# A smaller descriptor ring for GpSimd's transfers, and its memory given to one more probability tile of each kind and one more slot

## The chip, the cores and the metric

One core of one Trainium2 chip runs the kernel; the other cores are idle. The metric is the device time of one execution in microseconds (us). Engines are named as in the profile: PE (TensorE, the matrix unit) with its weight loads PEld, DVE (VectorE), ACT (ScalarE), POOL (GpSimd) and SP (SyncE, which only issues transfers here). Each engine runs its own instructions in the order in which the program has them, and waits where a semaphore says so.

## The reference, cut to what matters

One layer of a decoder over 1024 tokens of width 1024: a wide projection, three attention branches (a: dilated windows in three groups, b: compressed, selected and windowed blocks, c: a window of 128 with sinks), a gated sum of the three, an output projection and a layer norm. All in float32.

```python
h = x @ w_in[l] + b_in[l]
...
s = jnp.einsum('bnikgd,bnckd->bnkgic', qp.astype(jnp.float32), kc.astype(jnp.float32)) * ATTN_SCALE
s = s - (slopes.reshape(Hkv, G)[:, :, None, None] * dist_scale) * dist.astype(jnp.float32)
s = jnp.where(valid[None, :, None, None], s, NEG)
lse = jax.nn.logsumexp(s, axis=-1)
...
p = jnp.exp(s - lse[..., None])
o = jnp.einsum('bnkgic,bnckd->bnikgd', p, vc.astype(jnp.float32))
...
merged = (mg[:, :, 0] * (ya @ w_branch[l, 0])
          + mg[:, :, 1] * (yb @ w_branch[l, 1])
          + mg[:, :, 2] * (yc @ w_branch[l, 2]))
y = (merged @ w_out[l]).astype(x.dtype)
x = layer_norm(DEEPNORM_ALPHA * x + y, ln_g[l], ln_b[l])
```

## The kernel before, in words

The first 885 us or so are the **dense stage**: the projection, with its own pool of on-chip memory, and its results stored to memory on the chip's HBM. Then that pool is closed and the pool "ab" opened, with which all the rest works: branch a (head pairs p = 0 to 3, each with blocks b = 0 to 7), then branch c, then branch b, then the output projection. While branch c runs, PE's gaps are filled with the products of branch a's output with its branch weights (tile `dbr`, and `ma` for the gated sums), and while branch b runs with those of branch c; so a branch's outputs are needed again as soon as the next branch begins.

The work of one block and head pair is a *unit* with three parts, `front`, `mid` and `back` (`a_unit`, `b_unit`, `c_unit`). `front` puts scores into a PSUM bank (PE, L931 and L943 for a, L1029 for b and c); DVE adds the distance strip, takes the row's least value and writes the sum into a **probability tile** ("softmin", L681, tiles `ae`, `be`, `ce`); ACT exponentiates in place (L685); DVE or ACT scales by the reciprocal of the row sum (L690, L692). `mid` transposes the probabilities on PE (L970 and L972 for a, L1176 for c, L1139 for b; tiles `atp`, `atq`, `ctp`, `btp`) and copies them back into the slots (L163 on ACT, L165 on DVE; `apt`, `pt`). `back` multiplies them with the values (PE, L987, L994, L1070) and gates the result (`y`, L700 on DVE), which GpSimd stores to memory with its own transfers (L703). The lo parts of a split float32 operand are made on POOL (L179) from the hi parts that DVE or ACT casts (L173, L171).

Four things of the pool matter here. `slot` hands out 4 KB slots (tag "g", `NG` of them; queries, keys, values and transposed probabilities). `etile` hands out probability tiles of two kinds (tags "e0" and "e1", `NE` of each; an a or c unit takes one of each, its two heads, and a b unit two of each). A score bank is one of `NPS` = 4. A tile is handed out again when its last reader is done, and whoever writes it next waits for that reader: for a probability tile the reader is the transpose on PE, and the writer is DVE's softmin, or POOL's fill of the masked columns ahead of it (L928, `MEMSET`) or its copy of the sink (L1164).

The parts of the units are written down with two lags (`LAG_MID`, `LAG_BACK`), but the order of each engine's instructions is decided when the program is built, by the framework's scheduler, which plays the program with its own idea of durations and takes what is ready first; when a tile comes free is one of its inputs. So a change of the number of tiles can reorder every engine.

GpSimd issues 82 transfers in all: the stores of `y` of the three branches (`y_a` 8, `y_b` and `y_c` 16 each), of the merged sums `m` (40, L778) and two of `h`. Its descriptors go through a ring in on-chip memory, by default 16 KB of each partition. The program gives these transfers eight completion semaphores in turn, and a transfer on one of them waits for the one before it there, so that at most eight are under way. All other transfers are issued by SP and don't use this ring.

Of the kernel before, what the change touches and what calls it, by code (L numbers as in the profile page):

```python
# [101 lines left out]
B_STRIP = SEL_W + P + CMP_W  # L102


NG, NH, NE, NPS = 23, 36, 4, 4
LAG_MID, LAG_BACK = 3.5, 2.0
NWOP = 9
C1, C2 = 2, 4
# [1196 lines left out]
def build(arrays):  # L1305
    import concourse.bacc as bacc

    nc = bacc.Bacc("TRN2", target_bir_lowering=False, num_devices=1)
    args = [nc.dram_tensor(f"in_{n}", a.shape, mybir.dt.from_np(a.dtype), kind="ExternalInput").ap()
            for n, a in arrays.items()]  # L1310
    out = nc.dram_tensor("out_0", (S, D), F32, kind="ExternalOutput").ap()
    with tile.TileContext(nc, schedule_with_timeline_sim=True) as tc:
        trunk(tc, *args, out)
    return nc
# [39 lines left out]
```

## Time and profile before

| what | value |
|---|---|
| median of 3 runs | 1614.71 us (1611.72, 1614.71, 1619.58) |
| the profiled execution | 1612.14 us, of which 1610.3 us are its span (first to last instruction) |
| PE busy | 1565.2 us, 97% of the span |
| DVE, ACT, POOL busy | 61%, 48%, 41% |
| mean granted clock of PE | 0.992 |
| chain of waits | PE 85%, DVE 8%, issue 3%, ACT 2%, DMA 1% |

Busy shares are over the whole span; the dense stage, with more than half of it, is PE alone, and what lies behind it has other limits in other places. A stretch in which PE's busy time is near its length is bounded by PE; the difference is all that another arrangement of the work could give there, as long as PE's own work stays the same. The granted clock is a share of 2.4 GHz; 0.50 in a stretch is the lower level, 1.2 GHz.

### The profile page before, as it was taken

Reading aid. Unit: us, or ns where it says so; the run is one execution under the profiler, and the core shown is the slowest. Engines: PE = TensorE matmul, PEld = TensorE weight load, DVE = VectorE, ACT = ScalarE, POOL = GpSimd, SP = SyncE. Lnnn points to the kernel's source line nnn. Section 1 sums busy time; section 2 is a strip of 40 time slices with the busy share of each in tenths; the row PEclk is TensorE's granted clock in tenths of the full one; section 3 lists DMA queues with packets and bytes.
Section 4 is the critical chain, followed back from the end, with each engine's and each line's share of the span. In section 5 each row is a group of like instructions: output and inputs, shape, how many; then the busy total and the mean of one; then the engine's idle time right before and its main releaser. Section 6 shows DMA issues by size and latency. Waiting matters only on the chain.

```text
span 1610.3 us, 26460 instructions
## 1 busy us (share of the span) xinstructions
PE 1565.2 (97%) x9468; PEld 1260.1 (78%) x9468; DVE 978.8 (61%) x2325; ACT 774.4 (48%) x1628; POOL 659.3 (41%) x613
## 2 busy tenths in 40 slices
PE   8999999999999999999999999998989999999997
PEld 8888888888899988788788666766767767776786
DVE  8533335555733444844873777776586787778655
ACT  5444444444322233533543566664574576668422
POOL 0655555555555655565663101135335412210320
PEclk9999999999999999999999999999999999999999
DMA  4322332333443322522544776767536522312632
GB/s 163 131 105 105 123 119 112 118 131 131 172 129 112 105 105 105 209 105 105 209 171 182 258 252 215 244 228 241 191 112 229 190 105 62 125 65 92 230 124 79
DMA packets 104004, 241.08 MB, mean 150 GB/s; under 512 B 11456, under 2 KB 28608, under 8 KB 103872
## 3 DMA queue, kind: packets, MB, share of 16 engines
q1 hardware_dynamic: 98208, 221.56, 39.0%
q0 software_dynamic: 5664, 17.83, 2.9%
q8 instruction: 75, 1.23, 0.3%
q14 instruction: 57, 0.47, 0.1%
HBM read 154.94 MB, written 84.41 MB: 149 GB/s over the span
## 4 chain that ended last, share of the span: by engine, by line
PE 85%; DVE 8%; issue 3%; ACT 2%; DMA 1%; POOL 0%; SPq 0%; DVEq 0%; ACTq 0%; POOLq 0%
PE dn L192 13%; PE dn L190 13%; PE dn L191 13%; PE vn L491 8%; PE pv L1070 6%; PE bs L1029 4%; PE btp L1139 4%; PE dbr L190 3%; PE dbr L191 3%; PE dbr L192 3%; PE do L1227 2%; PE do L1226 2%; PE do L1228 2%; PE apv L994 1%; DVE ae L681 1%
## 5 line engine op out<-in xcount | busy, mean ns | idle before, releaser
L223 POOL TENSOR_TENSOR s<-s,s 128x512 fp32r<-128x512 f32 x147 | 201.8, 1374 | 267.3 <-ACT s L222 262.4
L190 PE MATMUL dn<-xh_t,s 128*128 128x512 f32 x456 | 177.6, 389 | 0.0
L192 PE MATMUL dn<-xh_t,s 128*128 128x512 f32 x456 | 177.5, 389 | 0.0
L191 PE MATMUL dn<-xl_t,s 128*128 128x512 f32 x456 | 177.4, 389 | 0.0
L223 POOL TENSOR_TENSOR a<-w,a 128x512 fp32r<-128x512 f32 x109 | 146.8, 1347 | 57.0 <-ACT a L222 41.1
L222 ACT CAST a<-w 128x512 fp32r<-128x512 f32 x114 | 70.8, 622 | 167.0 <-PE dn L192 133.3
L685 ACT ACTIVATE be<-be,mn 128x64 f32<-128x64 f32 (+8 forms) x192 | 115.2, 602 | 52.3 <-DVE mn L681 51.6
L190 PE MATMUL dn<-xh_b,a 128*128 128x512 f32 x288 | 113.4, 394 | 5.6 <-ACT c L412 5.6
L222 ACT CAST s<-s 128x512 fp32r<-128x512 f32 x152 | 93.8, 619 | 51.1 <-PE dn L192 34.0
L230 DVE TENSOR_TENSOR s<-w,s 128x512 f32<-128x512 f32 x38 | 30.5, 803 | 141.5 <-POOL s L223 139.7
L192 PE MATMUL dn<-xh_b,a 128*128 128x512 f32 x288 | 113.2, 393 | 0.0
L191 PE MATMUL dn<-xl_b,a 128*128 128x512 f32 x288 | 113.2, 393 | 0.0
L190 PEld LDWEIGHTS dn<-xh_t,s 128*128 128x128 f32 x456 | 85.7, 188 | 17.8
L192 PEld LDWEIGHTS dn<-xh_t,s 128*128 128x128 f32 x456 | 85.7, 188 | 17.8
L191 PEld LDWEIGHTS dn<-xl_t,s 128*128 128x128 f32 x456 | 85.6, 188 | 17.8
L1139 PE MATMUL btp<-ident,be 128*128 128x128 f32 x592 | 87.8, 279 | 2.4 <-DVE be L690 1.8
L228 DVE TENSOR_TENSOR s<-w 128x512 f32<-128x512 f32 x38 | 33.0, 867 | 84.1 <-POOL s L223 81.5
L1139 PEld LDWEIGHTS btp<-ident,be 128*128 128x128 f32 x592 | 68.3, 142 | 19.5 <-issue 8.0
L432 POOL TENSOR_TENSOR o<-c,c 128x512 f32<-128x512 f32 x38 | 64.9, 1708 | 26.0 <-issue 16.6
L681 DVE CUSTOM_DVE_ANT_0 be<-bs,con_b 128x512 f32<-128x512 f32 (+5 forms) x128 | 66.2, 530 | 8.0 <-PE bs L1029 7.9
L190 PEld LDWEIGHTS dn<-xh_b,a 128*128 128x128 f32 x288 | 54.7, 190 | 17.8 <-ACT c L412 6.4
L685 ACT ACTIVATE ae<-ae,mn 128x768 f32<-128x768 f32 (+2 forms) x64 | 51.8, 811 | 34.0 <-DVE mn L681 31.4
(309 smaller groups left out, 4258.2 us busy)
## 6 DMA issues: line engine op xcount, KB each, us to landing
w<-in_w SPq DMA_DIRECT2D x88, 512.0 KB, 4.4
h<-o SPq DMA_DIRECT2D x47, 512.0 KB, 3.7
h<-hi SPq DMA_DIRECT2D x38, 512.0 KB, 2.7
a<-h SPq DMA_DIRECT2D x48, 256.0 KB, 7.5
h<-gt SPq DMA_DIRECT2D x12, 512.0 KB, 2.6
h<-vo SPq DMA_DIRECT2D x24, 256.0 KB, 2.8
av<-h SPq DMA_DIRECT2D x12, 512.0 KB, 5.6
xr<-in_xt SPq DMA_DIRECT2D x8, 512.0 KB, 6.7
```

Of the source, the lines that this page charges most:

```text
L190: nc.tensor.matmul(ps, h, mh[k], start=(first and k == 0), stop=False, skip_group_check=True)
L191: nc.tensor.matmul(ps, h, ml[k], start=False, stop=False, skip_group_check=True)
L192: nc.tensor.matmul(ps, l, mh[k], start=False, stop=(last and k == n - 1), skip_group_check=True)
L222: nc.scalar.copy(hi[o], v)
L223: e.tensor_sub(lo[o], v, hi[o].bitcast(F32))
L432: nc.gpsimd.tensor_add(d, e, half(o2, 1, k2, tm["c5"])[1])
L491: nc.tensor.matmul(to, x_[b][k][:, at], w_[a][:, :, c], start=(first and t_ % 2 == k == i == 0), stop=(last and k == 3 and i == 2), skip_g ...
L681: nc.vector.tensor_tensor_reduce(e, ps, strip, scale, init, OP.add, OP.min, m)
L685: nc.scalar.activation(e, e, AF.Exp, bias=m, scale=-1.0, accum_out=den)
L1029: nc.tensor.matmul(pss[s], qs[s][:, bl], ks[2 * i + s][:, c0:c0 + n], start=(i == 0), stop=(i == 1))
L1070: nc.tensor.matmul(pv[64 * s:64 * s + 64, :, b % 2], v[s], state[b, s, j // w][:, j % w], start=(j == 0), stop=(j == len(vs) - 1), skip_gr ...
L1139: nc.tensor.transpose(tp[:, j], e[:, k:k + P], ident)
```

## The change

The ring of descriptors of GpSimd's transfers is 4096 bytes of each partition, not 16384. The 12 KB that come free hold one more slot (4 KB) and one more probability tile of each of the two kinds (4 KB for e0, whose largest tile has 1024 columns, 3 KB for e1, whose largest has 768). Nothing else in the text of the kernel changes.

```diff
-NG, NH, NE, NPS = 23, 36, 4, 4
+NG, NH, NE, NPS = 24, 36, 5, 4
...
-    nc = bacc.Bacc("TRN2", target_bir_lowering=False, num_devices=1)
+    nc = bacc.Bacc("TRN2", target_bir_lowering=False, num_devices=1, dynamic_dma_scratch_size=4096)
```

The order of the dense stage is the same on every engine. Behind it the scheduler orders the work otherwise in many places. Three of them follow.

**Branch a, head pair 2, DVE.** The rows stand where the last output of head pair 1 (`y_8618`) is gated between the softmins of head pair 2's blocks 4 and 5. `as1` are scores of the two dilated groups, `as0` those of the near group. Before:

```order
L681 ISA ae_8626,mn_8622<-as0_8647,ast21_8315,mn_8622 128x256
L681 ISA mn_8622 128x1
L165 COPY apt0_8500<-atp_8501 128x128
L165 COPY apt2011_8499<-atp_8508 128x128
L700 TENSOR_TENSOR y_8618<-apv11_8569,ag1_7705 128x4x4x32
L681 ISA ae_8685,mn_8682<-as0_8707,ast20_8311,mn_8682 128x256
L681 ISA mn_8682 128x1
L956 RECIPROCAL rc_8624<-den_8623 128x2
L690 TENSOR_SCALAR ae_8626<-ae_8626,rc_8624 128x768
L165 COPY apt2010_8498<-atp_8561 128x128
L681 ISA ae_8686,mn_8682<-as1_8688,ast21_8315 128x2x192
```

After the change, the same place:

```order
L681 ISA ae_8626,mn_8622<-as0_8647,ast21_8315,mn_8622 128x256
L681 ISA mn_8622 128x1
L681 ISA ae_8686,mn_8682<-as1_8688,ast21_8315 128x2x192
L681 ISA mn_8682 128x1
L165 COPY apt0_8500<-atp_8501 128x128
L165 COPY apt2011_8499<-atp_8508 128x128
L690 TENSOR_SCALAR ae_8518<-ae_8518,rc_8517 128x512
L681 ISA ae_8685,mn_8682<-as0_8707,ast20_8311,mn_8682 128x256
```

The softmin of block 5's second head (`as1_8688`) now stands ahead of two copies, the gate `y_8618` and a scale, and a scale of an older block (`ae_8518`) has come behind it: the softmins go first, the older blocks' scales and copies later.

**From branch a to branch c, DVE.** Here DVE casts branch a's outputs and weights (`wha1`) for the first branch products, copies the selected keys for branch b (`bsk`, L1018), and takes the softmins of branch c (`ce`). Before:

```order
L1018 COPY bsk0_11101<-kc0_408 128x64
L681 ISA ce_10175,mn_10170<-cs_10173,con_c_7667,nsink_66 128x256
L681 ISA mn_10170 128x1
L1018 COPY bsk1_11102<-kc1_409 128x64
L1168 RECIPROCAL rc_10133<-den_10132 128x2
L173 CAST wha1_10058<-wra1_10057 128x512
L690 TENSOR_SCALAR ce_10136<-ce_10136,rc_10133 128x256
L690 TENSOR_SCALAR ce_10137<-ce_10137,rc_10133 128x256
L681 ISA ce_10176,mn_10170<-cs_10174,con_c_7667,nsink_66 128x256
L681 ISA mn_10170 128x1
L1018 COPY bsk2_11103<-kc2_410 128x64
```

After the change:

```order
L1018 COPY bsk0_11101<-kc0_408 128x64
L1018 COPY bsk1_11102<-kc1_409 128x64
L1168 RECIPROCAL rc_10133<-den_10132 128x2
L173 CAST wha1_10058<-wra1_10057 128x512
L690 TENSOR_SCALAR ce_10136<-ce_10136,rc_10133 128x256
L690 TENSOR_SCALAR ce_10137<-ce_10137,rc_10133 128x256
L1018 COPY bsk2_11103<-kc2_410 128x64
L681 ISA ce_10175,mn_10170<-cs_10173,con_c_7667,nsink_66 128x256
L681 ISA mn_10170 128x1
L1018 COPY bsk3_11104<-kc3_411 128x64
L681 ISA ce_10176,mn_10170<-cs_10174,con_c_7667,nsink_66 128x256
```

The softmin of `cs_10173` has moved behind the cast of `wha1`, the two scales and a copy, and that of `cs_10174` behind two copies more. Fewer rows stand ahead of `wha1`, more ahead of the two softmins.

**From branch c to branch b, PE.** `dbr_11537` is the first of branch c's branch products, which needs DVE's cast `yhc0_11481`; `btp` are transposes of branch b's probabilities, `bs1` and `bs2` scores. Before:

```order
L1139 MATMUL btp_11396<-ident_63,be2_11266 128x128
L190 MATMUL dbr_11537<-yhc0_11481,whc0_11466 128x512
L1029 MATMUL bs1_11561<-bsk0_11101,bq100_11130 128x448
L1029 MATMUL bs1_11561<-bsk2_11103,bq100_11130 128x448
L1029 MATMUL bs1_11562<-bsk1_11102,bq110_11133 128x448
L1029 MATMUL bs1_11562<-bsk3_11104,bq110_11133 128x448
L1029 MATMUL bs2_11571<-bwk0_11113,bq100_11130 128x384
L1029 MATMUL bs2_11571<-bwk2_11115,bq100_11130 128x384
L1139 MATMUL btp_11447<-ident_63,be1_11340 128x128 x2
```

After the change:

```order
L1139 MATMUL btp_11396<-ident_63,be2_11266 128x128
L1139 MATMUL btp_11447<-ident_63,be1_11340 128x128 x2
L1139 MATMUL btp_11447<-ident_63,be2_11341 128x128 x2
L1139 MATMUL btp_11453<-ident_63,be2_11341 128x128
L1139 MATMUL btp_11456<-ident_63,be1_11342 128x128 x2
L1139 MATMUL btp_11456<-ident_63,be2_11343 128x128 x2
L190 MATMUL dbr_11537<-yhc0_11481,whc0_11466 128x512
L1029 MATMUL bs1_11561<-bsk0_11101,bq100_11130 128x448
```

Nine transposes of the next block now stand ahead of the branch product. On DVE the five scales on which these transposes wait (`be1_11340` to `be2_11343`, L690) stand ahead of the cast `yhc0_11481`, and before they stood right behind it.

## Rows read from the trace of the kernel before

**Rows 1.** The page: the chain that ended last, by engine.
```profile
PE 85%; DVE 8%; issue 3%; ACT 2%; DMA 1%; POOL 0%; SPq 0%; DVEq 0%; ACTq 0%; POOLq 0%
```

**Rows 2.** Stretches: length; busy PE, PEld, DVE, ACT, POOL; PE clock, DMA share, GB/s.
```profile
935.00:983.00 48.00, 46.86 (x718) 35.21 (x720) 32.11 (x137) 26.97 (x71) 4.05 (x14) 1.00 0.64 227
983.00:1022.00 39.00, 36.26 (x530) 26.86 (x522) 27.57 (x112) 24.25 (x65) 4.38 (x14) 1.00 0.72 242
1022.00:1062.00 40.00, 38.33 (x416) 28.36 (x416) 27.95 (x106) 27.04 (x76) 4.72 (x19) 1.00 0.44 150
1062.00:1100.00 38.00, 31.16 (x166) 23.28 (x166) 32.42 (x113) 22.95 (x79) 20.28 (x38) 0.91 0.80 292
1100.00:1172.00 72.00, 71.66 (x394) 53.40 (x392) 41.72 (x146) 38.28 (x121) 26.36 (x61) 1.00 0.67 223
1172.00:1200.00 28.00, 23.73 (x137) 16.82 (x135) 25.55 (x128) 22.79 (x87) 8.58 (x9) 0.94 0.23 81
1200.00:1480.00 280.00, 276.54 (x1687) 199.56 (x1688) 210.99 (x748) 178.46 (x458) 79.18 (x83) 1.00 0.35 114
```

**Rows 3.** The same view in stretches of 20 us, branch a.
```profile
980.00:1000.00 20.00, 17.82 (x245) 12.27 (x244) 19.54 (x81) 17.74 (x47) 2.12 (x7) 1.00 0.44 144
1000.00:1020.00 20.00, 19.45 (x288) 15.51 (x288) 8.86 (x36) 6.73 (x19) 2.26 (x7) 1.00 1.01 347
1020.00:1040.00 20.00, 18.09 (x247) 12.29 (x246) 19.71 (x83) 18.41 (x48) 2.47 (x8) 1.00 0.43 143
```

**Rows 4.** DVE's timeline: start, us, line, operation, idle time before and its releaser.
```profile
978.12 0.29 DVE L681 CUSTOM_DVE_ANT_1 ae<-as,ast 128x128 f32<-128x128 f32 x1 [4.88 <-PE as L931]
```

**Rows 5.** PE's timeline, head pair 2 of branch a.
```profile
989.22 1.36 PE L931 MATMUL as<-ak,aq 64*32 64x224 f32 x30 [0.71 <-DVE mn L681]
...
1000.04 0.44 PE L972 MATMUL atq<-ident,ae 128*128 128x128 f32 x2 [1.16 <-DVE apt L165]
```

**Rows 6.** Waits of 935 to 1480 us, all engines: total, times, longest.
```profile
POOL ae L928 <- PE atp L972: 35.1, 6, 16.0
```

**Rows 7.** DVE's timeline from branch a to branch c.
```profile
1087.13 0.47 DVE L681 CUSTOM_DVE_ANT_0 ce<-cs,con_c,nsink 128x256 f32<-128x256 f32 x1
...
1088.44 1.45 DVE L173 CAST wha<-wra 128x512 fp32r<-128x512 f32 x1
1089.82 2.65 DVE L690 TENSOR_SCALAR ce<-ce,rc 128x256 f32<-128x256 f32 x2
1092.38 0.47 DVE L681 CUSTOM_DVE_ANT_0 ce<-cs,con_c,nsink 128x256 f32<-128x256 f32 x1
...
1092.79 0.86 DVE L1018 CAST bsk<-kc 128x64 fp32r<-128x64 f32 x1
```

**Rows 8.** PE's timeline, and POOL's, in the same place.
```profile
1089.95 0.50 PE L190 MATMUL dbr<-ya,wha 128*128 128x512 f32 x1 [2.01 <-DVE wha L173]
...
1092.92 0.80 PE L1029 MATMUL cs<-ck,cq 128*128 128x256 f32 x2 [1.55 <-DVE mn L681]
...
1081.59 9.45 POOL L179 TENSOR_TENSOR ya<-yra,ya 128x512 fp32r<-128x512 f32 x7
```

**Rows 9.** PE's and DVE's timelines from branch c to branch b.
```profile
1189.66 0.50 PE L190 MATMUL dbr<-yhc,whc 128*128 128x512 f32 x1 [2.82 <-DVE yhc L173]
...
1189.18 0.42 DVE L173 CAST yhc<-yrc 128x512 fp32r<-128x512 f32 x1
1189.52 2.35 DVE L690 TENSOR_SCALAR be<-be,rc 128x256 f32<-128x256 f32 x5
```

**Rows 10.** GpSimd's transfers: queue; issues, shortest/median/longest ns, first to last; landing.
```profile
q0 software_dynamic: 5664, 17.83, 2.9%
...
L703 POOL DMA_DIRECT2D y_c<-y x16: 539/540/562, 1074.0 to 1180.5; - x16
...
L778 POOL DMA_DIRECT2D m<-ma x16: 539/542/559, 1094.5 to 1164.3; - x16
...
m<-ma POOLq DMA_DIRECT2D x16, 256.0 KB, 3.4
```

## The prediction

> **What bounds the kernel now.** I read the chain of waits first: it is PE for 85% and DVE for 8% [rows 1]. The dense stage, whose order the change leaves alone, is the larger part of the time. Then I cut what lies behind it into stretches [rows 2] and subtract PE's busy time from the length of each. Branch a from 935 us on: 1.1, 2.7 and 1.7 us idle. From a to c, 1062 to 1100 us: 6.8. Branch c: 0.3. From c to b, 1172 to 1200 us: 4.3. Branch b to 1480 us: 3.5. The sum is 20.4 us, and this is the ceiling of what another order of the same work can give back, 1.3% of the time, but for the clock: two stretches ran at 0.91 and 0.94 of full speed, which is 0.09 × 38 + 0.06 × 28 = 3.4 + 1.7 = 5.1 us more. With it the ceiling is 25.5 us.
>
> Next, which engine holds PE up there. In stretches of 20 us, branch a's DVE alternates between full and nearly empty: 19.54 of 20, then 8.86, then 19.71 [rows 3]. PE's idle time falls into the full ones. So in these DVE is the bound, and a wait that names DVE is a wait for DVE's throughput and not for one late instruction. Last, who waits for the tiles that the change adds: POOL, which waits up to 16.0 us for the transposes that free a tile before it fills the next [rows 6]. POOL is busy for 4 to 5 us of each 40 there [rows 2]; its waits cost something only where DVE's softmin is late for them.
>
> **The change part by part.** *Branch a.* One more tile of each kind lets a block's softmins go earlier, by as much as one block. The order shows it: in head pair 2 the softmin of block 5 stands ahead of the gate and a scale. Two waits should shrink or go: PE's 0.71 us for a score bank at 989.22 us, which the earlier softmin frees, and the same one of head pair 3. But DVE does the same work in another order. It began its full half at 978.12 us, after 4.88 us of waiting for PE's scores [rows 4], and the order of PE's rows ahead of those scores is the same in both programs; so the full half starts when it did. It ends with a copy for which PE waits 1.16 us at 1000.04 us [rows 5], and with DVE busy for 19.54 of 20 us the copy can come earlier only by what DVE idles: 0.46 us there and 0.29 us in the next full half [rows 3]. I take that, −0.75 us for head pairs 2 and 3. For head pair 1, PE idles 1.1 us in all of 935 to 983 us; I take half of it, −0.5. The bounds are 0 and the whole idle time of the branch, −5.5 us.
>
> *From a to c.* Here POOL makes seven lo parts one after another, 9.45 us from 1081.59 us on [rows 8], and meanwhile DVE's operations are slow: two scales of 128x256 take 2.65 us [rows 7], where five take 2.35 from c to b [rows 9]. PE waits 2.01 us for the cast of `wha`, then 1.55 us for a softmin [rows 8]. The change takes one softmin, 0.47 us at 1087.13 us, from ahead of the cast, whose start at 1088.44 us moves up by about 0.4 us. Then it puts that softmin and one to two copies of `bsk` (0.86 us each at 1092.79 us) ahead of the softmin that ended PE's second wait [rows 7]. If PE waits for the first of the two softmins, its score is freed at 1092.38 − 0.4 + 0.86 + 0.47, which is 1093.3 us, against 1092.9 before: +0.4. If it waits for the second, a further copy and softmin come first, +1.3 to +1.7. I take +0.5 as the sum of this place, near the lower end since POOL is done at about that time. Queued behind the waiting scores on PE are the branch products and transposes of branch c; they are late by the same amount. PE's clock fell to the lower level about here (0.91 over the stretch, after PE's waits of 2.01 and 1.55 us), and a longer wait could keep it there: as an upper bound as much as the clock takes now, 3.4 us, comes again, which with 1.7 is +5.1. The lower bound is −3.6, both waits gone.
>
> *From c to b.* PE's wait of 2.82 us for the cast `yhc` at 1189.66 us looks like what the new order mends, since nine transposes now stand ahead of that product. But the scales on which those transposes wait took 2.35 us right behind the cast, from 1189.52 us on, and now stand right ahead of it [rows 9]. PE's next instruction thus waits for the first scale, which ends about when the cast ended before (both follow the same DVE work, one cast of 0.42 us apart); and the product then waits for the cast behind five scales. DVE is busy for 25.55 of 28 us there. I take 0. The bounds are −4.3 − 1.7 = −6.0 (all of PE's idle time and the clock) and +2.4 (the five scales in the way of the cast, if the transposes find something else missing).
>
> *Branch b.* PE idles 3.5 of 280 us. A b unit holds two tiles of each kind, so the fifth is half a block of lead. I take −0.5, between 0 and −3.5.
>
> *The slot.* Loads of keys and values may start one place earlier; each of PE's waits shown here ends with DVE and none with a load [rows 5, 8, 9], so it is 0: the loads lie beside the units' work. Without that cover it would be worth the landing of a load, some 3 us as for a store of 256 KB [rows 10].
>
> *The smaller ring.* 82 transfers are 5664 packets, 69 for each [rows 10]. At most eight are under way, 552 packets. POOL spends 0.54 us on each issue; if descriptors still find a place, that stays, and I take 0. If they don't, the price is that of the second rival, below.
>
> The Trainium skill speaks against this edit: its page "Debugging Trainium Hangs", section "Descriptor Overflow", puts hangs down to too many descriptors for the SBUF carveout on the Pool queue, and a quarter of the carveout would come to that point with a quarter of the descriptors. By "DMA: Bandwidth & Descriptors", section "Terms", a descriptor has 16 bytes, so that 4096 bytes would hold 256; 552 packets over the 16 engines are 35 for each, an estimate by which the ring stays far from full. No row here shows how full a ring is.
>
> The sum is −0.75 − 0.5 + 0.5 + 0 − 0.5 = −1.25 us. The profiled execution took 1612.14 us, so the changed one should take 1610.9. The median of the runs, 1614.71, is 2.6 us more; with that difference the prediction is 1613.5 us. Less than 0.5%, 8 us, can't be told from no change here, since the three runs before differ by 7.9 us.
>
> **The rivals.** *Faster: the lead evens DVE out.* If the softmins of the next head pair slide into the light halves, where DVE has 11 us free of 20, the full halves stop holding PE, and the same happens at the two transitions. Recovering 40% to all of the 25.5 us gives 1587 to 1602 in the profile, on the median's scale 1589 to 1604. For it speaks that the waits are where the tiles are used; against it, that DVE's full half waits for PE's scores at its start [rows 4], which no tile brings forward. Chance 0.20.
>
> *Slower: the ring is too small.* If an issue must wait until an older transfer has been read, POOL stands still for up to a landing, 3.4 us instead of 0.54 [rows 10], 2.9 us more for each. Branch b has the time for it: POOL is busy for 79 of 280 us, and some 40 transfers would add 116. Branch c just has it: 16 stores of `ma` would bring POOL from 26.4 to 73 us of 72 [rows 2, 10]. The transitions don't: the first stores of `y_c` stand on POOL ahead of the seven lo parts at 1081.59 us, the last among the lo parts of branch c's output [rows 8, 10], and behind POOL's lo parts queue PE's products. With two issues in the way at the one place and two at the other, that is 4 × 2.9 = 11.6 us, and I put +8 to +15, so 1622 to 1630 us with the 2.6 from above. It is decided at the point where the descriptors of the transfers under way no longer fit the ring; that only eight of 82 can be under way speaks against it. The Trainium skill's page "Debugging Trainium Hangs" (section "Descriptor Overflow") names the same cause, with a hang where I price a stall. Chance 0.07.
>
> *Slower: the new order hurts the transitions.* The upper bounds above come together: +5.1 from a to c, +2.4 and once more the clock's 1.7 from c to b, which is 9.2 us, 1623.9 on the median's scale. For it speaks that the softmins do move behind slow copies; against it, that each of PE's waits there is under 3 us. Chance 0.10.
>
> *Nothing happens:* tiles are late nowhere that counts, and reordering cancels out, 1614.7 us. Chance 0.18. My forecast has 0.45.
>
> **The numbers.** Forecast and nothing lie within 0.5%: 0.63. Faster by over 0.5% is the first rival, 0.20; slower the other two, 0.17. The range reaches into both sides so far that about half of each is left out: 1603 to 1623 us.
>
> **What would show it.** Right: stretches of equal length to within 1 us up to the end of branch a, the 0.71 us waits gone but DVE still full for its halves; POOL's issues at 0.54 us; `wha` earlier and the wait for branch c's scores longer. Wrong: a full half of DVE that begins after much less than those 4.88 us of waiting, PE idle from 1172 to 1200 us well under 4 us, or issues on POOL of several us.

## The result, and the profile after

The changed kernel takes 1634.68 us (median of 5 runs, 1632.82 to 1635.5), the kernel before 1614.71 beside it (5 runs, 1611.72 to 1619.58). The ratio is 1.0121, with an interval of 1.0102 to 1.014: slower by 20 us, outside the forecast range of 1603 to 1623. The profiled execution has a span of 1632.9 us, 22.6 more than before, and a mean clock of 0.983. Executions of one kernel scatter (23 of the kernel before, run beside the first experiments, lie between 1611.59 and 1620.45 us), and the profiled one of before is near the lower end, so a difference between two profiles is good to a few microseconds only.

The page of the changed kernel, busy time by engine and the chain by engine (the latter answers to [rows 1]):

```profile
PE 1578.1 (97%) x9468; PEld 1266.5 (78%) x9468; DVE 982.3 (60%) x2325; ACT 775.7 (48%) x1628; POOL 657.7 (40%) x613
...
PE 85%; DVE 7%; ACT 2%; issue 2%; DMA 2%; SPq 1%; POOL 0%; DVEq 0%; ACTq 0%; POOLq 0%
```

DVE has lost a point and DMA has gained one; shares over the whole span don't say more. The stores do, because they mark the stages. GpSimd's issues after (count: shortest/median/longest ns, first to last start), which answer to [rows 10]:

```profile
L703 POOL DMA_DIRECT2D y_a<-y x8: 539/543/617, 938.5 to 1083.0; - x8
L703 POOL DMA_DIRECT2D y_c<-y x16: 539/542/609, 1094.0 to 1202.9; - x16
L703 POOL DMA_DIRECT2D y_b<-y x16: 539/542/637, 1232.6 to 1519.8; - x16
L778 POOL DMA_DIRECT2D m<-ma x16: 539/542/559, 1115.3 to 1185.2; - x16
```

Of before, the rows of `y_c` and `m` are in [rows 10], and those of `y_a` and `y_b` are

```profile
L703 POOL DMA_DIRECT2D y_a<-y x8: 539/540/1024, 924.3 to 1064.3; - x8
L703 POOL DMA_DIRECT2D y_b<-y x16: 539/542/774, 1211.5 to 1498.2; - x16
```

Subtracting milestone from milestone gives where the 22.6 us arose:

| stretch | before | after | difference | forecast |
|---|---|---|---|---|
| start to first `y_a` | 924.3 | 938.5 | +14.2 | 0 |
| first to last `y_a` (branch a) | 140.0 | 144.5 | +4.5 | −1.25 |
| last `y_a` to first `m` (a to c) | 30.2 | 32.3 | +2.1 | +0.5 |
| first to last `m` (branch c) | 69.8 | 69.9 | +0.1 | 0 |
| last `m` to first `y_b` (c to b) | 47.2 | 47.4 | +0.2 | 0 |
| first to last `y_b` (branch b) | 286.7 | 287.2 | +0.5 | −0.5 |
| last `y_b` to the end | 112.1 | 113.1 | +1.0 | 0 |

Nearly two thirds lie ahead of the first store, a stretch of which the prediction shows no row. Stretches of after, each begun as much later than in [rows 2] as the work is late there (15 to 21 us; same columns):

```profile
950.00:999.00 49.00, 46.23 (x708) 34.68 (x704) 31.56 (x134) 26.38 (x68) 4.32 (x14) 1.00 0.60 212
999.00:1039.00 40.00, 37.27 (x547) 27.87 (x548) 28.71 (x118) 25.72 (x70) 4.06 (x14) 1.00 0.70 246
1039.00:1081.00 42.00, 40.64 (x397) 28.77 (x397) 29.80 (x111) 29.39 (x83) 4.92 (x20) 0.96 0.42 132
1081.00:1121.00 40.00, 29.94 (x164) 22.19 (x165) 31.58 (x98) 20.64 (x68) 19.23 (x36) 0.91 0.80 294
1121.00:1193.00 72.00, 71.95 (x393) 53.41 (x392) 42.13 (x147) 37.70 (x118) 26.06 (x59) 1.00 0.68 220
1193.00:1221.00 28.00, 24.65 (x142) 16.93 (x142) 24.86 (x124) 21.99 (x86) 8.43 (x9) 0.94 0.18 60
1221.00:1502.00 281.00, 276.00 (x1681) 199.25 (x1681) 212.20 (x753) 180.98 (x462) 79.34 (x84) 1.00 0.37 123
```

In branch a PE idles 2.8, 2.7 and 1.4 us (before 1.1, 2.7 and 1.7), and its clock is 0.96 in the last of the three. From a to c it idles 10.1 us (40 less 29.94), where it idled 6.8; from c to b 3.4 (before 4.3), and in branch b 5.0 of 281 (before 3.5 of 280).

**Ahead of the first store.** Of the 14.2 us, 3.6 arise in the dense stage, whose order the change leaves alone: SyncE's last stores there start at 870.20 us and not at 866.62. In the profiled execution PE, never idle, ran at 0.89 of its clock from 30 to 60 us; seven of the seventeen kernels profiled here show this in their profiled execution, and the other ten, that of before among them, don't. Whether the changed kernel's four other executions had it isn't on record. The rest begins where pool "ab" takes over the memory of the dense stage. SyncE's timeline before (start, us, line, loads) and after:

```profile
875.36 3.73 SPq L141 DMA_DIRECT2D a<-h  x6
...
886.75 0.59 SPq L141 DMA_DIRECT2D pos<-in_pos  x1
```

```profile
880.31 9.21 SPq L141 DMA_DIRECT2D a<-h  x6
...
895.91 0.63 SPq L141 DMA_DIRECT2D pos<-in_pos  x1
```

Six loads of 256 KB took 3.73 us to issue and now take 9.21. SyncE issues in order, so values, gates, keys, positions and weights behind them are late as well, and PE at the end of that row (PE's timeline before, then after):

```profile
898.39 0.67 PE L828 MATMUL ph<-w,cst 128*126 128x256 f32 x2 [0.84 <-DVE cst L826]
```

```profile
908.05 1.22 PE L828 MATMUL ph<-w,cst 128*126 128x256 f32 x2 [4.07 <-DVE cst L826]
```

`cst` is worked out from `pos`, whose load was issued 9.2 us later (895.91 against 886.75); the product that needs it begins 9.7 us later, 6.1 of which are the change's and 3.6 the dense stage's. PE waits 4.07 us, and its clock is down for longer. Stretches of 10 us, before and after (the last columns are clock, DMA share, GB/s):

```profile
890.00:900.00 10.00, 8.40 (x78) 5.84 (x66) 7.90 (x36) 6.62 (x21) 0.99 (x6) 0.66 1.04 366
900.00:910.00 10.00, 10.00 (x111) 7.17 (x110) 5.22 (x24) 5.50 (x16) 0.30 (x2) 1.00 0.95 314
```

```profile
890.00:900.00 10.00, 7.25 (x111) 5.13 (x112) 6.16 (x33) 3.74 (x9) 1.88 (x9) 0.71 0.95 314
900.00:910.00 10.00, 5.48 (x37) 3.51 (x35) 4.90 (x22) 4.23 (x14) 0.85 (x5) 0.50 1.06 307
910.00:920.00 10.00, 10.00 (x63) 6.27 (x59) 2.85 (x12) 2.83 (x7) 0.00 (x0) 0.60 0.95 326
```

A mean of 0.66 over 10 us is 6.8 us at 1.2 GHz (each us there is missing 0.5). After it is 5.8 + 10 + 8 = 23.8 us. The DMA share is 0.95 and more in all these rows, so there is little room to make up for a late start; this is an argument, which no run tests. The 14.2 us are thus 3.6 of the dense stage, 6.1 by which the product that waits for `cst` is later still, and, as what is left, 4.5 of clock and waits.

**Why these six loads wait.** SyncE's order, two loads of that row and the semaphores that they wait for. Before, and then after:

```
242 L141 DMA a_000_7066<-h_0_6293 128x512 [waits DMAHW1_49,PE_49]
243 L141 DMA a_001_7067<-h_1_6294 128x512 [waits DMAHW2_49]
```

```
242 L141 DMA a_000_7066<-h_0_6293 128x512 [waits DMAHW1_49,PE_49]
243 L141 DMA a_001_7067<-h_1_6294 128x512 [waits DMAHW2_49,PE_49]
```

The instruction and its place are the same; one wait for PE is new. The largest tile that `slot` hands out has 1088 columns, so a slot is 4352 bytes (and not 4 KB). A 24th slot moves everything behind it in pool "ab" by 4352 bytes against the dense pool, whose memory it reuses. By the addresses in the two programs, the second load of `a` lay on a weights tile that was read early, and now lies on `s4_64`, an operand of the sixth of the dense stage's last seven groups of products, read until 2.7 us before its end (12 products of 0.23 us follow). That this shift is the cause was a theory at this point; its rival was that the order of the units, with more tiles, brings PE's needs and the loads into conflict.

### The profile page after: what moved, and what is told of

It is laid out like the page before. It is cut to its first block, busy times and chain, and to the rows that moved or that the text cites. A ratio compares the mean times of both kernels' runs of the same rounds, so it can differ in the third digit from the quotient of the medians.

```text
span 1632.9 us, 26411 instructions
## 1 busy us (share of the span) xinstructions
PE 1578.1 (97%) x9468; PEld 1266.5 (78%) x9468; DVE 982.3 (60%) x2325; ACT 775.7 (48%) x1628; POOL 657.7 (40%) x613
## 4 chain that ended last, share of the span: by engine, by line
PE 85%; DVE 7%; ACT 2%; issue 2%; DMA 2%; SPq 1%; POOL 0%; DVEq 0%; ACTq 0%; POOLq 0%
PE dn L190 13%; PE dn L192 13%; PE dn L191 13%; PE vn L491 7%; PE pv L1070 6%; PE bs L1029 4%; PE btp L1139 4%; PE dbr L190 3%; PE dbr L191 3%; PE dbr L192 3%; PE do L1227 2%; PE do L1228 2%; PE do L1226 2%; PE apv L994 1%; DVE ae L681 1%
## 5 line engine op out<-in xcount | busy, mean ns | idle before, releaser
L192 PE MATMUL dn<-xh_b,a 128*128 128x512 f32 x288 | 113.1, 393 | 0.0
```

The costliest lines, as they stand in the source:

```text
L192: nc.tensor.matmul(ps, l, mh[k], start=False, stop=(last and k == n - 1), skip_group_check=True)
```

## The experiments

All kernels but the thirteenth run have the ring of 4096 bytes; the diffs leave that line out from the second run on. No kernel leaves out any part of the computation; where a pool is shifted, an unused tile is added, of which one column is filled. The ratios and their intervals are those on record; they aren't the quotients of the medians beside them, from which they differ by up to 0.17%.

**The parts alone.** The first run (`e1_ring_alone`) changes the ring and nothing else:

```diff
-    nc = bacc.Bacc("TRN2", target_bir_lowering=False, num_devices=1)
+    nc = bacc.Bacc("TRN2", target_bir_lowering=False, num_devices=1, dynamic_dma_scratch_size=4096)
```

> Only the ring is 4 KB; slots and probability tiles as before, and every engine's order is that of before. Place theory (the loss comes from where the 24th slot pushes the memory of the attention stage against that of the dense stage, so that its first loads wait for the dense stage's last products): no change, 1610 to 1620 us. Ring theory (GpSimd's transfers suffer from the small ring): about +20 us, near 1635. Order theory (the fifth probability tiles reorder the engines for the worse): no change.

Measured: 1616.07 against 1616.97 us, ratio 0.9996 (0.9979 to 1.0014). The ring has no cost that can be measured.

The second (`e2_tiles_alone`) has the fifth tiles without the slot:

```diff
-NG, NH, NE, NPS = 23, 36, 4, 4
+NG, NH, NE, NPS = 23, 36, 5, 4
```

> Ring 4 KB and five probability tiles of each kind, but 23 slots, so that the first loads of the attention stage lie on the same tiles of the dense stage as before. Place theory: within 5 us of before, 1608 to 1618 us, first store of y_a at 924 us as before. Ring theory: +20. Order theory: most of the +20, with the loss between the first store of y_a and the end.

Measured: 1620.27 against 1616.97, ratio 1.0037 (1.0022 to 1.0053).

The third (`e3_slot_alone`) has the slot without the tiles:

```diff
-NG, NH, NE, NPS = 23, 36, 4, 4
+NG, NH, NE, NPS = 24, 36, 4, 4
```

> Ring 4 KB and 24 slots, but four probability tiles of each kind. Place theory: most of the loss, +10 to +20 us (1625 to 1635), the first store of y_a near 935 us or later and PE at the lower clock for 15 us or more around 905 to 930 us. Ring theory: +20. Order theory: within 5 us of before.

Measured: 1625.35 against 1616.97, ratio 1.0064 (1.0041 to 1.0086). So there are two losses, and the slot's is the larger.

**The place in memory.** The fourth (`e4_both_moved_back`) is the whole change, with the dense pool moved by the same 4352 bytes, so that the two pools lie against each other as before:

```diff
-NG, NH, NE, NPS = 23, 36, 4, 4
+NG, NH, NE, NPS = 24, 36, 5, 4
     dp = dpool.__enter__()
+    nc.vector.memset(dp.tile([P, 1088], F32, tag="pad", name="dpad", bufs=1)[:, :1], 0.0)
```

> The whole change, and an unused tile of 4352 bytes at the start of the dense stage's memory, which puts the first loads back onto the tiles of the dense stage that they lay on before; the order of the engines is that of the changed kernel. Place theory: the loss is gone, 1608 to 1618 us. Ring theory and order theory: still near 1635 us.

Measured: 1626.37 against 1616.97, ratio 1.0065 (1.0044 to 1.0087). Only about half of the loss is gone: the place is one cause of at least two. Its first `y_a` is 2.8 us later than before's, and what is left lies in branch a, 147.3 us (before 140.0), and from a to c, 32.2 us (before 30.2):

```profile
L704 POOL DMA_DIRECT2D y_a<-y x8: 542/542/614, 927.1 to 1074.4; - x8
```

The fifth (`e5_shift_alone`) is the other way round: 23 slots, 4 tiles, the order of before on every engine but for the fill, and pool "ab" shifted:

```diff
     ap = pool("ab", bufs=2)
+    nc.vector.memset(ap.tile([P, 1088], F32, tag="pad", name="apad", bufs=1)[:, :1], 0.0)
```

> Slots, tiles, ring and the order of every engine are those of before; an unused tile of 4352 bytes (the size of one slot) lies ahead of the attention stage's memory, so that this memory is pushed against the dense stage's as with 24 slots. Place theory: the whole loss of the slot-alone run comes back, +8 to +11 us, the first store of y_a 8 to 9 us late. Rival (the 24th slot costs by the order that it brings, not by the place): no change.

Measured: 1623.88 against 1615.87, ratio 1.006 (1.0043 to 1.0077). With no slot, no tile and no reordering the kernel loses 0.6%. This is the run that shows the shift as a cause by itself. Its dense stage is undisturbed, and its first `y_a` starts at 936.3 us, 12.0 later than before; branch a then takes 140.0 us, as before. SyncE's waits for the last dense products (us in total, times, longest), before and then in this run, and this run's stores of `y_a`:

```profile
SPq L141 <- PE dn L192: 4.5, 5, 3.3
```

```profile
SPq L141 <- PE dn L192: 11.2, 3, 6.5
L704 POOL DMA_DIRECT2D y_a<-y x8: 542/542/1022, 936.3 to 1076.3; - x8
```

The sixth (`e6_slot_moved_back`) has 24 slots and 4 tiles, with the dense pool moved by 4352 bytes; the ninth (`e9_half_back`) has the same with 2048, which is just enough to give that one load another place:

```diff
-NG, NH, NE, NPS = 23, 36, 4, 4
+NG, NH, NE, NPS = 24, 36, 4, 4
     dp = dpool.__enter__()
+    nc.vector.memset(dp.tile([P, 1088], F32, tag="pad", name="dpad", bufs=1)[:, :1], 0.0)   # sixth
+    nc.vector.memset(dp.tile([P, 512], F32, tag="pad", name="dpad", bufs=1)[:, :1], 0.0)    # ninth
```

> 24 slots, four probability tiles, the order of the slot-alone run, and an unused tile of 4352 bytes at the start of the dense stage's memory, which puts the first loads back. Place theory: within 3 us of before. Rival (order): +8 to +11 as in the slot-alone run.

> 24 slots, four probability tiles, the order of the slot-alone run, and an unused tile of only 2048 bytes at the start of the dense stage's memory. That moves one load, of half a near query, off the dense stage's operand that is read in the sixth of its last seven product groups; the other loads still lie off their places of before. If this one load's wait is the cause: as in the slot-moved-back run, within 4 us of before. If the push as a whole costs: about half of the slot-alone run's loss or more, +5 us or over.

Measured: 1618.6 against 1615.87, ratio 1.0023 (1.0007 to 1.0039), and 1620.06 against 1616.97, ratio 1.0025 (1.0009 to 1.0042). The same waits of SyncE in the third, the sixth and the ninth:

```profile
SPq L141 <- PE dn L192: 11.1, 3, 6.1
```

```profile
SPq L141 <- PE dn L192: 4.4, 3, 3.3
```

```profile
SPq L141 <- PE dn L192: 5.2, 4, 4.0
```

The wait of 6.1 us comes and goes with the shift, 2048 bytes are as good as 4352 by the ratios, and about 0.4% of time goes with it (1.0064 against 1.0023). Single profiles can't tell the two amounts apart: the first `y_a` of the ninth starts at 932.7 us, but its clock was down from 30 to 60 us, and in the seventh run (below), which has that too and no shift, it starts at 932.2. What is left of the slot, 0.23%, is not settled; the sixth's profiled execution has a span of 1611.0 us, 0.7 more than before's, and no stretch of it is more than 1.2 us longer.

**The tiles.** The seventh (`e7_e0_alone`) gives the fifth tile to the first kind only:

```diff
-        return ap.tile([P, n], F32, tag=f"e{i}", name=name, bufs=NE)
+        return ap.tile([P, n], F32, tag=f"e{i}", name=name, bufs=NE + 1 - i)
```

> 23 slots; five tiles of kind e0 but four of e1. A block of branch a or c takes one of each, so it gets no lead there; branch b may begin half a block earlier. If the loss of the tiles-alone run comes from the lead in branch a: the same time as before to the end of branch a, and within 3 us of before at the end. If any reordering costs: +3 us or more, spread over branch b.

Measured: 1616.66 against 1615.87, ratio 1.0004 (0.9986 to 1.0021): no loss. The fifth tile of the first kind doesn't make it by itself; that of the second kind alone was not run.

The eighth (`e8_three_tiles`) goes the other way, `NE` = 3:

```diff
-NG, NH, NE, NPS = 23, 36, 4, 4
+NG, NH, NE, NPS = 23, 36, 3, 4
```

> 23 slots and three probability tiles of each kind, less lead than before. If more lead makes branch a slower because the softmins push back the copies that free the transposes' banks, less lead should not slow branch a by that, so PE's waits for these copies stay at before's 2 to 3 us, but waits for softmins grow: -2 to +6 us. If tiles are plainly what limits, every stage gets slower by more than the fifth tile did: over +6 us.

Measured: 1637.43 against 1615.87, ratio 1.0143 (1.0123 to 1.0163). Its stores show where:

```profile
L703 POOL DMA_DIRECT2D y_a<-y x8: 539/542/1024, 930.5 to 1068.9; - x8
L703 POOL DMA_DIRECT2D y_b<-y x16: 539/539/699, 1219.1 to 1520.4; - x16
```

Branch a takes 138.4 us there (before 140.0): even three tiles are enough for it. It is branch b, whose unit takes two of each kind, that loses: 301.3 us from first to last `y_b`, before 286.7.

So branch a does not need more tiles; why does it lose with five? PE's waits in branch a, 924 to 1083 us, after, and then with the tiles alone (the second run), and before (924 to 1065 us):

```profile
PE atp L970 <- DVE apt L165: 3.2, 5, 0.9
PE atp L970 <- ACT apt L163: 2.1, 3, 1.4
PE atq L972 <- ACT apt L163: 1.3, 3, 0.8
```

```profile
PE atp L970 <- DVE apt L165: 4.3, 7, 1.2
PE atq L972 <- ACT apt L163: 3.7, 3, 2.0
...
PE atp L970 <- ACT apt L163: 0.2, 1, 0.2
```

```profile
PE atq L972 <- DVE apt L165: 1.2, 1, 1.2
PE atp L970 <- DVE apt L165: 0.8, 1, 0.8
...
PE atq L972 <- ACT apt L163: 0.5, 1, 0.5
PE atp L970 <- ACT apt L163: 0.5, 2, 0.3
```

PE's transposes wait 3.0 us for the copies that empty their PSUM banks before, 6.6 after and 8.2 with the tiles alone. Not all of the loss is waiting: between the first and the last `y_a` PE idles 6.2 us before, 7.9 after and 9.3 with the tiles alone, and in both of the slower kernels it is also busy for 2.8 us longer, at a mean clock of 0.99 and 0.98 against 1.00. The theory: with a tile in hand DVE takes the next softmin first, and the copies, which free the three transposes' banks (`NPR` = 3), come later. Its rival: this is one unlucky order, and any other does without the loss. The tenth and eleventh (`e10_tiles_less_lag`, `e11_tiles_more_lag`) keep five tiles and change when a unit's middle part is due:

```diff
-NG, NH, NE, NPS = 23, 36, 4, 4
-LAG_MID, LAG_BACK = 3.5, 2.0
+NG, NH, NE, NPS = 23, 36, 5, 4
+LAG_MID, LAG_BACK = 2.5, 2.0    # tenth
+LAG_MID, LAG_BACK = 4.5, 2.0    # eleventh
```

> 23 slots, five tiles of each kind, and the transposes of a block are written one unit of lag earlier in the program (2.5 and not 3.5). If the tiles' loss is that softmins push the copies out of the transposes' banks back: PE's waits for these copies in branch a (8 us in the tiles-alone run) shrink to 4 us or less, and the time is 1612 to 1619 us. If not: as in the tiles-alone run or slower, 1620 us or over.

> As the run before, but with a lag of 4.5. If the copies that come late are the cause: more of their waits, 1622 us or over. If the fifth tile only wanted a longer lag: under 1616 us.

Measured: 1617.37 and 1618.01 against 1616.97, ratios 1.0 (0.9979 to 1.0021) and 1.0012 (0.9993 to 1.0032). The shorter lag, which puts the copies earlier, removes the loss, as the theory has it; but the longer one does too, and it was expected to cost at least as much. PE's waits for the copies from 924 to 1083 us come to 3.8 us with the shorter lag and 4.3 with the longer, against 8.2: both orders have fewer of them, which fits the copies as the cause, and what failed is the expectation that a longer lag brings more of them. So the rival has its share: the loss belongs to this order and is no price of a fifth tile. One trace doesn't fit: the profiled execution of the tenth, the slowest of its ten at 1628.14 us, takes 145.8 us for branch a (930.0 to 1075.8) in spite of its few waits, at a mean clock of 0.94. The other nine have no trace.

The twelfth (`e12_tiles_four_banks`) gives the transposes a fourth bank, taken from the scores; the thirteenth (`e13_banks_alone`) does this to the kernel before, with its ring of 16 KB:

```diff
-NG, NH, NE, NPS = 23, 36, 4, 4
+NG, NH, NE, NPS = 23, 36, 5, 3    # twelfth
+NG, NH, NE, NPS = 23, 36, 4, 3    # thirteenth
-NPR = 3
+NPR = 4
```

> 23 slots, five tiles of each kind; one more PSUM bank for transposes (four) and one fewer for scores (three). If late copies are the cause: PE's waits for copies in branch a fall under 4 us, those for score banks rise; time between 1612 and 1622 us. If the waits for the copies stay at about 8 us, the bank is not what they wait for.

> The kernel before, ring and tiles as before, with four PSUM banks for transposes and three for scores. If the fourth bank gives by itself what the run with five tiles and four banks gained in branch a: y_a 4 us or more earlier across branch a and 1614 to 1618 us in all. If the banks only help where the fifth tile has pushed the copies back: no gain in branch a, or a loss by score banks, 1617 us or over.

Measured: 1617.19 against 1616.97, ratio 1.0004 (0.9985 to 1.0023), and 1629.14 against 1615.81, ratio 1.0087 (1.006 to 1.0114). The stores of `y_a` of the second, twelfth and thirteenth runs, and `y_b` of the last:

```profile
L703 POOL DMA_DIRECT2D y_a<-y x8: 542/544/1032, 923.7 to 1069.6; - x8
```

```profile
L703 POOL DMA_DIRECT2D y_a<-y x8: 542/644/944, 929.9 to 1064.4; - x8
```

```profile
L703 POOL DMA_DIRECT2D y_a<-y x8: 539/542/1867, 925.2 to 1060.9; - x8
L703 POOL DMA_DIRECT2D y_b<-y x16: 539/539/604, 1215.1 to 1513.0; - x16
```

Branch a takes 145.9 us with five tiles and three banks, 134.5 with four banks; with four tiles it takes 140.0 and 135.7. So five tiles cost branch a 5.9 us while three banks serve the transposes, and nothing with four: the banks are where the tiles' loss arises. PE's waits for the copies are gone in the twelfth run, and those for score banks are 2.1 us, where the second run has 0.3. Part of what the fourth bank gives branch a is lost right behind it: from the last `y_a` to the first `m` the twelfth run takes 35.0 us and the thirteenth 36.9, against 30.2 before and 29.7 with the tiles alone. From the first `y_a` to the first `m` the reading is the same: five tiles cost 5.4 us with three banks (175.6 against 170.2) and give 3.1 with four (169.5 against 172.6). The fourth bank is no gift by itself, since branch b, left with three score banks, takes 297.9 us in the thirteenth run against 286.7. There the fifth tile pays: with the same banks and five tiles branch b takes 289.6 us, and the whole 1617.19 against 1629.14.

**Both mended.** The fourteenth (`e14_all_mended`) is the whole change with the dense pool moved back and the fourth bank; the fifteenth (`e15_banks_less_lag`) is the twelfth with the shorter lag:

```diff
-NG, NH, NE, NPS = 23, 36, 4, 4
+NG, NH, NE, NPS = 24, 36, 5, 3    # fourteenth
+NG, NH, NE, NPS = 23, 36, 5, 3    # fifteenth
-LAG_MID, LAG_BACK = 3.5, 2.0
+LAG_MID, LAG_BACK = 2.5, 2.0      # fifteenth
-NPR = 3
+NPR = 4
     dp = dpool.__enter__()
+    nc.vector.memset(dp.tile([P, 1088], F32, tag="pad", name="dpad", bufs=1)[:, :1], 0.0)   # fourteenth
```

> The whole change (ring, 24 slots, five tiles), with the first loads put back by the unused tile of 4352 bytes and with four banks for transposes and three for scores. If the three causes add up (place +9 us, tiles +6, the slot's rest +3), the first two are gone: 1616 to 1622 us. If the banks don't mend the tiles' part here: near 1626 us, as without them.

> 23 slots, five tiles, four banks for transposes, lag 2.5. Both edits by themselves took the tiles' loss away. If the copies were the only fault of the five tiles: no better than either, 1615 to 1619 us. If each left a part of it: under 1614 us.

Measured: 1618.92 against 1615.81, ratio 1.0006 (0.9982 to 1.0031), and 1618.13 against 1615.81, ratio 1.0026 (1.0003 to 1.0049). With both causes taken away the change's loss is gone from the whole, though not stage by stage: in the fourteenth's profiled execution (1618.14 us) branch a takes 135.9 us (before 140.0), from a to c 35.7 (30.2) and branch b 290.0 (286.7). By the ratios no version here is faster than the kernel before (the ring alone, 0.9996, can't be told from it): the 12 KB, spent in this way, buy nothing.

## Why the prediction was wrong, step by step

By the ratios, the shift (1.0060), the tiles (1.0037) and the rest of the slot (1.0023) add to 1.20%, against the measured 1.21%. That these meet so closely is luck: each interval is some 0.15% wide to either side, and the differences of the medians, 8.0, 3.3 and 2.7 us, add to 14.0 of 20.0 us. The share of the place by itself scatters too: it is 0.60% by the fifth run, 0.41% by the third against the sixth, and 0.56% by the change against the fourth, so 7 to 10 us.

**The slot: 0, covered by PE's own work.** This step failed, and it is the larger error. It rested on rows from 989 us on, in which no wait of PE ends with a load. The prediction shows none between 880 and 935 us, where the chain of before has a load in it (the chain of waits, before):

```profile
886.75 11.09 DMA pos<-in_pos
```

There the cover is thin: the DMA share is 1.04 from 890 to 900 us, and in the fifth run, where only the place changed, the first `y_a` came 12.0 us late. The remark that the dense stage's order is left alone was true, and it misled: what the change moved was not an instruction but the address of a tile. The ceiling had the same gap, since it began at 935 us; a loss has no ceiling of that kind anyway.

**Branch a: −0.75 − 0.5.** The sign was wrong, +4.5 in the profile (+5.9 with the tiles alone). The parts that I had read were right: DVE's full half begins after the same wait as in [rows 4] (DVE's timeline, after),

```profile
994.50 0.29 DVE L681 CUSTOM_DVE_ANT_1 ae<-as,ast 128x128 f32<-128x128 f32 x1 [4.88 <-PE as L931]
```

and the two waits of 0.71 us for a score bank [rows 5] are gone. What failed is that "the copy can come earlier only by what DVE idles", which took it that no copy would come later. DVE does the same work in another order, so what a softmin gains another instruction loses; it was the copies, and PE's transposes wait for these.

**From a to c: +0.5.** The place and the sign were right, the size off: +2.1. PE's two waits, 2.01 and 1.55 us, have become one of 4.67 us, which ends with a softmin, as forecast; the product that waits takes its bank from the same four as the scores. But the cast of `wha` gained nothing: it starts 5.5 us after the first branch product that waits for POOL's lo part (1102.78 us), as before (1082.90 us). PE's timeline after, and DVE's:

```profile
1113.93 0.79 PE L190 MATMUL dbr<-ya,wha 128*128 128x512 f32 x1 [4.67 <-DVE mn L681]
```

```profile
1109.69 2.62 DVE L690 TENSOR_SCALAR ce<-ce,rc 128x256 f32<-128x256 f32 x2
1112.23 1.25 DVE L1018 CAST bsk<-kc 128x64 fp32r<-128x64 f32 x1
1113.39 0.47 DVE L681 CUSTOM_DVE_ANT_0 ce<-cs,con_c,nsink 128x256 f32<-128x256 f32 x1
```

The softmin stands behind two scales and a copy that takes 1.25 us and not 0.86 [rows 7]; my lower bracket (+0.4) was taken where the upper (+1.3 to +1.7) was the nearer. With the tiles alone this stretch takes 29.7 us (1069.6 to 1099.3, first `m`) and with the slot alone 30.2, so slot and tiles make it together.

**From c to b: 0.** Right: +0.2. The product that waited 2.82 us [rows 9] waits no more, and the transposes that now stand ahead of it wait in its place (PE's timeline after):

```profile
1207.46 1.52 PE L1139 MATMUL btp<-ident,be 128*128 128x128 f32 x10 [0.66 <-DVE be L690]
1210.71 1.55 PE L1139 MATMUL btp<-ident,be 128*128 128x128 f32 x9 [1.73 <-ACT be L685]
1211.91 0.79 PE L190 MATMUL dbr<-yhc,whc 128*128 128x512 f32 x1
```

**Branch b: −0.5.** Measured +0.5; the half block of lead bought nothing.

**The ring: 0.** Right: ratio 0.9996 (0.9979 to 1.0014) alone, and GpSimd's issues keep their median of 0.54 us in the changed kernel. The rival of a ring too small falls, and with it what the Trainium skill's page "Debugging Trainium Hangs" (section "Descriptor Overflow") warned of, for transfers of this size and number.

**The rivals.** The one that ends on the slower side by its transitions had 2.3 us of its 9.2, nearly all from a to c. The forecast's other sides, faster and nothing, are out. None of the cases had a load that is late at the change of pools, and none had copies that come later; these two are the loss.

Three things stay open: the slot's rest of 0.23%, why a longer lag also shortens the waits for the copies, and how the 14.2 us ahead of the first store divide. The 4.5 us of clock and waits are a remainder. Five kernels whose clock was down from 30 to 60 us and whose first loads lie where they lay have their first `y_a` at 929.2 to 932.2 us, 4.9 to 7.9 later than before, so of the changed kernel's 14.2 us some 6 to 9 are the change's.

## What to carry to other kernels

A change of a buffer's count or size moves every tile behind it in its pool; where that pool reuses the memory of an earlier one, compare the waits of the first loads in the two programs, not only the order of instructions. One load that waits holds all those behind it on an issuing engine that works in order, and what it costs is read from the first microseconds after the change of pools. Where a scheduler takes what is ready first, one more buffer for a producer can put the producer's work first, and the question is whose buffers are then emptied later: here PSUM banks of another part of the same unit.

## What the runs showed of the hardware

A wait that came to some 6 us on SyncE's queue, for one transfer of 256 KB, cost 7 to 10 us of the whole. With it PE, after waits of 4.07 us and less, was at 1.2 GHz for 23.8 us and not 6.8; in the fifth run its granted clock was 0.50 from 890 to 910 us. A ring of 4096 bytes carried 82 transfers of GpSimd with at most eight under way at no cost that can be measured (0.9996, 0.9979 to 1.0014). And in seven of seventeen profiles, of kernels with the same dense stage, the granted clock was 0.89 from 30 to 60 us, with PE busy throughout; in the others it was at 1.00. The changed kernel's row:

```profile
30.00:60.00 30.00, 30.00 (x144) 25.61 (x144) 25.68 (x37) 14.04 (x25) 11.45 (x8) 0.89 0.25 88
```
